# One pool of three PSUM banks for dense products and layer norms, in place of two and one

## The chip, the cores and the metric

The kernel runs on one core of a Trainium2 chip. Its time is the device time of one execution, in microseconds (us); of the kernel before it is the median of three runs. The core's engines are TensorE (PE in the rows; PEld is its weight load), VectorE (DVE), ScalarE (ACT), GpSimd (POOL) and SyncE (SP), which here issues the DMAs. TensorE writes its results to PSUM, which this kernel divides into eight banks of 128 partitions by 512 fp32 values.

## The reference

Two layers, each made of a half-step SwiGLU, a token mixer, and a second half-step SwiGLU. Behind each of the three stands a layer norm, and that is the part of the reference that this change touches.

```python
def layer_norm(x, g, b):
    xf = x.astype(jnp.float32)
    mu = xf.mean(-1, keepdims=True)
    var = jnp.square(xf - mu).mean(-1, keepdims=True)
    return ((xf - mu) * lax.rsqrt(var + LN_EPS)).astype(x.dtype) * g + b

def swiglu(h, w_in, w_out):
    gate, up = jnp.split(h @ w_in, 2, axis=-1)
    return (jax.nn.silu(gate) * up) @ w_out

    # in reference(), h is (1, 576, 1024), of which 528 rows are live
    for l in range(DEPTH):                                    # DEPTH = 2
        h = layer_norm(DEEPNORM_ALPHA * h + 0.5 * swiglu(h, w_ff1_in[l], w_ff1_out[l]), ln_g[l, 0], ln_b[l, 0])
        mix = hybrid_mixer(h * valid, w_in[l], w_out[l], ...)  # 4 DeltaNet, 4 RWKV-7 and 4 retention heads
        h = layer_norm(DEEPNORM_ALPHA * h + mix, ln_g[l, 1], ln_b[l, 1])
        h = layer_norm(DEEPNORM_ALPHA * h + 0.5 * swiglu(h, w_ff2_in[l], w_ff2_out[l]), ln_g[l, 2], ln_b[l, 2])
```

## The kernel before

The 528 live tokens are cut into two halves of 272 and 256. Activations lie with the model dimension on the partitions, so a half is a tile `h` of 128 x 8 x 272 or 256. All work on a half is cut into units. A dense unit (`gate`, `up`, `ffo` of the SwiGLU; `qkv`, `rw`, `rt`, `z`, `ba`, `out` of the mixer) loads a 512 KB slab of weights (`raw`, four buffers), splits it into a high and a low fp32r part (`whl`, three buffers; ScalarE writes the high part at L127, VectorE the low part at L115), and runs 24 matmuls at L165 into one PSUM bank (18 where the slab is smaller): high by high, high by low and low by high, for up to eight slices of 128. This is called a product below. Then ScalarE and VectorE read the bank and so set it free: `gate` by a tanh and a `scalar_tensor_tensor` that writes `m`, `up` by a multiply with `m`, `ffo` and `out` by a `scalar_tensor_tensor` that adds to `h`.

The layer norm of a half is the function `layer_norm`. GpSimd has summed the eight slices of `h` into `acc` (`add_r`). One matmul with a matrix of ones makes the sums for the mean (`pmean`); four instructions of VectorE subtract the mean from `h`; ScalarE squares; VectorE and GpSimd add the squares (`sq`); four small matmuls make the variance (`pvar`); ten short VectorE instructions make the reciprocal root and a last one the diagonal matrix `diag`; one matmul spreads that over the partitions (`prs`); then VectorE and ScalarE scale `h` and write its high and low parts `hi` and `lo`, 16 instructions on VectorE. There are twelve layer norms: three for each layer and half. The last one of the second half has an `end` form, which leaves the last slice of `acc` to a second matmul and no work to GpSimd.

The banks: the dense products take theirs from `psA` (two), the three results of the layer norm from `psL` (one), the mixer's small products from `psB` (two) and `psC` (three).

What sets the order: the program is written as a sequence of units of both halves (`go`, `mix`, `turns`), so that units of one half stand behind a layer norm of the other. A scheduler then lays the instructions out for each engine when the kernel is built. A matmul can be laid out only once the pool of its tile has a bank free. On the chip each engine works through its own list.

Of the kernel before, what the change touches and what calls it, by code (L numbers as in the profile page):

```python
# [14 lines left out]
PSUM = bass.MemoryType.PSUM  # L15
# [44 lines left out]
def body(ctx, tc, xT, w1i, w1o, w2i, w2o, win, wba, wout, par, wsm, wupx, cst, tab, out):  # L60
# [7 lines left out]
    wh = ctx.enter_context(tc.tile_pool(name="whl", bufs=3))  # L68
    wk = ctx.enter_context(tc.tile_pool(name="work", bufs=1))
    st = ctx.enter_context(tc.tile_pool(name="state", bufs=1))  # L70
    psA = ctx.enter_context(tc.tile_pool(name="psA", bufs=2, space=PSUM))
    psL = ctx.enter_context(tc.tile_pool(name="psL", bufs=1, space=PSUM))
    psB = ctx.enter_context(tc.tile_pool(name="psB", bufs=2, space=PSUM))
    psC = ctx.enter_context(tc.tile_pool(name="psC", bufs=3, space=PSUM))
    dr = ctx.enter_context(tc.tile_pool(name="dram", bufs=1, space=DRAM))
# [1276 lines left out]
```

## Time and profile before

| | us |
|---|---|
| median of three runs (2446.88 to 2451.85) | 2447.68 |
| the profiled execution's own time | 2447.37 |
| its span, first to last instruction | 2445.5 |
| TensorE busy in the span | 2387.8 |
| VectorE busy | 1817.1 |
| ScalarE busy | 1226.5 |
| GpSimd busy | 293.7 |

The mean granted clock of TensorE is 0.993 of 2.4 GHz. The rows below come from one profiled execution. A row of the chain of waits gives a start in us, a length in us and what ran. A line such as L165 is that of a helper which many places call, so the names of the tiles tell what an instruction belongs to. A matmul of fp32 (`pmean`, `pvar`, `prs`) shows as two rows, so that 12 layer norms show 24 rows of `pmean`.

### The profile page before, as it was taken

How to read it: one execution, taken by the hardware profiler on the slowest of the kernel's cores; microseconds unless marked ns; L12 is line 12 of the kernel's file. 1: busy time of each engine (PE TensorE's matmuls, PEld its weight loads, DVE VectorE, ACT ScalarE, POOL GpSimd, SP SyncE). 2: the span in 40 equal slices, each digit the busy share in tenths (PEclk: the TensorE clock that was granted, in tenths of full speed). 3: DMA queues.
4: the chain of work that ended last, by engine and by line, in shares of the span. 5: the costliest groups of instructions: out<-in, count | busy, mean ns of one | idle time of the engine just before them, and what ended most of it. 6: DMA issues, size and time to landing. Idle time of an engine off the chain costs nothing.

```text
span 2445.5 us, 51826 instructions
## 1 busy us (share of the span) xinstructions
PE 2387.8 (98%) x20058; PEld 2285.6 (93%) x20058; DVE 1817.1 (74%) x4325; ACT 1226.5 (50%) x2813; POOL 293.7 (12%) x492
## 2 busy tenths in 40 slices
PE   9999999999899999999999999999999999999997
PEld 9999999889899989999999998889998989999997
DVE  6658688768888656976667679976688886687667
ACT  5445555434665334554445556633556653355444
POOL 1001112202222000300001003210022220010002
PEclk9999999999999999999999999999999999999998
DMA  7655554424544525555555544343455445255554
GB/s 248 207 166 172 182 165 134 130 90 157 174 156 150 144 87 172 178 171 179 179 179 172 191 159 153 118 121 107 163 174 190 156 143 154 93 194 170 194 168 127
DMA packets 169821, 389.24 MB, mean 159 GB/s; under 512 B 63750, under 2 KB 79720, under 8 KB 168936
## 3 DMA queue, kind: packets, MB, share of 16 engines
q1 hardware_dynamic: 169576, 385.94, 49.2%
q8 instruction: 158, 2.59, 0.4%
q14 instruction: 87, 0.71, 0.1%
HBM read 372.01 MB, written 13.88 MB: 158 GB/s over the span
## 4 chain that ended last, share of the span: by engine, by line
PE 89%; DVE 6%; DMA 2%; ACT 1%; issue 1%; POOL 1%; SPq 0%; POOLq 0%; DVEq 0%; ACTq 0%
PE up L165 20%; PE ffo L165 20%; PE gate L165 20%; PE qkv L165 6%; PE rw L165 3%; PE out L165 3%; PE rt L165 2%; DVE whl L115 2%; PE po L130 1%; DVE h L118 1%; PE z L165 1%; PE pR L130 1%; PE pyr L130 1%; PE pS L130 1%; PE pz L130 1%
## 5 line engine op out<-in xcount | busy, mean ns | idle before, releaser
L127 ACT ACTIVATE whl<-raw 128x512 fp32r<-128x512 f32 x1384 | 780.1, 614 | 620.6 <-issue 223.3
L115 DVE TENSOR_TENSOR whl<-raw,whl 128x512 fp32r<-128x512 f32 x1384 | 940.5, 710 | 94.4 <-ACT whl L127 79.4
L165 PE MATMUL gate<-hi,whl 128*128 128x256 f32 (+1 forms) x2816 | 553.3, 287 | 6.2 <-DVE m L118 4.0
L165 PE MATMUL up<-hi,whl 128*128 128x256 f32 (+1 forms) x2816 | 553.4, 287 | 2.7 <-DVE m L115 1.2
L165 PE MATMUL ffo<-ghi,whl 128*128 128x256 f32 (+1 forms) x2816 | 529.8, 286 | 5.4 <-DVE h L118 5.2
L165 PEld LDWEIGHTS gate<-hi,whl 128*128 128x128 f32 x2816 | 449.2, 189 | 13.7 <-DVE m L118 5.1
L165 PEld LDWEIGHTS up<-hi,whl 128*128 128x128 f32 x2816 | 450.6, 189 | 8.6 <-issue 3.7
L165 PEld LDWEIGHTS ffo<-ghi,whl 128*128 128x128 f32 x2816 | 440.4, 188 | 11.8 <-DVE h L118 6.4
L165 PE MATMUL up<-lo,whl 128*128 128x256 f32 (+1 forms) x1408 | 403.3, 286 | 0.0
L165 PE MATMUL gate<-lo,whl 128*128 128x256 f32 (+1 forms) x1408 | 402.0, 285 | 0.7 <-DVE lo L115 0.7
L165 PE MATMUL ffo<-glo,whl 128*128 128x256 f32 (+1 forms) x1408 | 399.2, 284 | 0.0
L165 PEld LDWEIGHTS gate<-lo,whl 128*128 128x128 f32 x1408 | 265.4, 188 | 3.8 <-issue 1.6
L165 PEld LDWEIGHTS up<-lo,whl 128*128 128x128 f32 x1408 | 266.4, 189 | 2.6 <-issue 1.2
L165 PEld LDWEIGHTS ffo<-glo,whl 128*128 128x128 f32 x1408 | 264.8, 188 | 0.9 <-issue 0.2
L127 ACT ACTIVATE tanh<-gate 128x256 f32<-128x256 f32 (+1 forms) x176 | 68.2, 387 | 229.8 <-PE gate L165 229.7
L118 DVE SCALAR_TENSOR_TENSOR m<-tanh,gate 128x256 f32<-128x256 f32 (+1 forms) x176 | 74.6, 424 | 139.5 <-ACT tanh L127 138.6
L118 DVE SCALAR_TENSOR_TENSOR h<-ffo,h 128x256 f32<-128x256 f32 (+1 forms) x192 | 81.5, 427 | 99.6 <-PE ffo L165 98.8
L165 PE MATMUL qkv<-hi,whl 128*128 128x272 f32 (+1 forms) x768 | 152.3, 290 | 1.6 <-ACT rk L127 1.6
L115 DVE TENSOR_TENSOR m<-m,up 128x256 f32<-128x256 f32 (+1 forms) x176 | 74.6, 424 | 95.7 <-PE up L165 95.3
L165 PEld LDWEIGHTS qkv<-hi,whl 128*128 128x128 f32 x768 | 122.4, 188 | 4.4 <-ACT rk L127 2.4
L165 PE MATMUL qkv<-lo,whl 128*128 128x272 f32 (+1 forms) x384 | 109.3, 285 | 0.0
L165 PE MATMUL out<-yhi,whl 128*128 128x256 f32 (+1 forms) x512 | 95.8, 285 | 4.6 <-DVE h L118 3.1
(316 smaller groups left out, 3271.1 us busy)
## 6 DMA issues: line engine op xcount, KB each, us to landing
raw<-w1i SPq DMA_DIRECT2D x176, 512.0 KB, 3.4
raw<-w2i SPq DMA_DIRECT2D x176, 512.0 KB, 3.3
raw<-win SPq DMA_DIRECT2D x116, 512.0 KB, 3.3
raw<-w1o SPq DMA_DIRECT2D x64, 512.0 KB, 3.3
raw<-w2o SPq DMA_DIRECT2D x64, 512.0 KB, 3.3
raw<-wout SPq DMA_DIRECT2D x32, 512.0 KB, 4.3
raw<-w1o SPq DMA_DIRECT2D x32, 384.0 KB, 3.0
raw<-w2o SPq DMA_DIRECT2D x32, 384.0 KB, 3.1
```

The costliest lines, as they stand in the source:

```text
L115: e.tensor_tensor(out=o, in0=a, in1=b, op=op)
L118: V.scalar_tensor_tensor(out=o, in0=a, scalar=s, in1=b, op0=op0, op1=op1)
L127: A.activation(out=o, in_=a, func=f, **kw)
L130: PE.matmul(o, lhsT=l, rhs=r, start=start, stop=stop)
L165: PE.matmul(ps, lhsT=w[:, a, k, :m], rhs=x[b][:, k, :n], start=(i == 0), stop=(i == 3 * nk - 1))
```

## The change

The pool `psL` goes away as a pool of its own: the name now stands for `psA`, which has three banks instead of two. The sum stays eight banks. The layer norm's three tiles (`pmean`, `pvar`, `prs`) and a few matmuls at the very start ask for their banks in the same pool as the dense products.

```diff
-    psA = ctx.enter_context(tc.tile_pool(name="psA", bufs=2, space=PSUM))
-    psL = ctx.enter_context(tc.tile_pool(name="psL", bufs=1, space=PSUM))
+    psA = psL = ctx.enter_context(tc.tile_pool(name="psA", bufs=3, space=PSUM))
     psB = ctx.enter_context(tc.tile_pool(name="psB", bufs=2, space=PSUM))
     psC = ctx.enter_context(tc.tile_pool(name="psC", bufs=3, space=PSUM))
```

No instruction is added or removed, but the lists change. Since the diff is one line shorter, line numbers of the changed kernel are one less (L129 for L130, L164 for L165).

TensorE's list at the first layer norm (first layer, half of 272), before: the matmul of the mean stands inside an `up` product of the other half.

```order
L165 MATMUL up<-hi,whl 128x256 x2
L165 MATMUL up<-lo,whl 128x256
L130 MATMUL pmean<-acc,ones 128x272
L165 MATMUL up<-hi,whl 128x256 x2
L165 MATMUL up<-lo,whl 128x256
```

It stands 32 matmuls behind the last `ffo` product that it follows from: a `gate` of 24 and eight of this `up` have been laid between.

Further down the same list, before, the matmul that spreads the root: it is the first thing between an `up` and a `gate` product. Between `pmean` and it the list has 160 matmuls of dense products.

```order
L165 MATMUL up<-hi,whl 128x256 x2
L165 MATMUL up<-lo,whl 128x256
L165 MATMUL up<-hi,whl 128x256
L130 MATMUL prs<-diag,ones 128x272
L165 MATMUL gate<-hi,whl 128x256
L165 MATMUL gate<-lo,whl 128x256
```

The variance's four matmuls stand in between in the same way, inside another `up`.

The same layer norm in TensorE's list of the changed kernel, from the last matmuls of the `ffo` products that it normalises.

```order
L164 MATMUL ffo<-ghi,whl 128x272 x2
L164 MATMUL ffo<-glo,whl 128x272
L164 MATMUL ffo<-ghi,whl 128x272
L129 MATMUL pmean<-acc,ones 128x272
L129 MATMUL pvar<-ones,sq 68x1 x4
L129 MATMUL prs<-diag,ones 128x272
L164 MATMUL gate<-hi,whl 128x256
L164 MATMUL gate<-lo,whl 128x256
```

The three kinds of matmul now stand one behind the other, with no dense product between them; the 160 matmuls stand behind `prs`. It is so at ten of the twelve layer norms. At the seventh (first layer, second SwiGLU, half of 256) thirteen small matmuls of the mixer stand between them and no dense product. The twelfth, the last work of the kernel, had nothing between them before either.

VectorE's list at the same layer norm, before, from the subtraction of the mean to the first adding of squares: splits of weights (`whl`) and work on products of the other half (`m`, `glo`) stand between.

```order
L118 SCALAR_TENSOR_TENSOR h<-pmean,h 128x544 x4
L115 TENSOR_TENSOR whl<-raw,whl 128x512
L115 TENSOR_TENSOR m<-m,up 128x256
L115 TENSOR_TENSOR whl<-raw,whl 128x512 x2
L115 TENSOR_TENSOR sq<-sq 128x544
L115 TENSOR_TENSOR glo<-m,ghi 128x256
L118 SCALAR_TENSOR_TENSOR m<-tanh,gate 128x256
```

The layer norm's steps and those of the other half alternate.

The same place in the changed kernel, from the last `ffo` result on.

```order
L117 SCALAR_TENSOR_TENSOR h<-ffo,h 128x272
L114 TENSOR_TENSOR whl<-raw,whl 128x512 x2
L117 SCALAR_TENSOR_TENSOR h<-pmean,h 128x544 x4
L114 TENSOR_TENSOR sq<-sq 128x544 x2
L114 TENSOR_TENSOR sq<-sq 128x272
L123 TENSOR_SCALAR var<-pvar 68x4
```

From the mean to `diag` VectorE's list holds nothing but this layer norm. Then come its 16 scaling instructions, and only behind them the first work on a dense product:

```order
L114 TENSOR_TENSOR diag<-cst,ry 68x272
L117 SCALAR_TENSOR_TENSOR h<-h,par_228,prs 128x272 x8
L117 SCALAR_TENSOR_TENSOR lo<-h,par_228,hi 128x272 x8
L117 SCALAR_TENSOR_TENSOR m<-tanh,gate 128x256
L114 TENSOR_TENSOR whl<-raw,whl 128x512 x2
```

The work on dense products, which was mixed in before, has moved behind all of these.

## Rows read from the trace of the kernel before

**Rows 1.** The page, its first lines: span, and busy time of each engine.

```profile
span 2445.5 us, 51826 instructions
PE 2387.8 (98%) x20058; PEld 2285.6 (93%) x20058; DVE 1817.1 (74%) x4325; ACT 1226.5 (50%) x2813; POOL 293.7 (12%) x492
```

**Rows 2.** The page, the chain that ended last: shares of the span by engine.

```profile
PE 89%; DVE 6%; DMA 2%; ACT 1%; issue 1%; POOL 1%; SPq 0%; POOLq 0%; DVEq 0%; ACTq 0%
```

**Rows 3.** Waits of TensorE: who for whom; us in total, times, longest us.

```profile
PE ffo L165 <- DVE h L118: 5.2, 9, 2.6
PE rt L165 <- DVE rt L115: 4.9, 3, 3.0
PE gate L165 <- DVE m L118: 4.0, 5, 1.7
PE out L165 <- DVE h L118: 3.1, 6, 1.0
PE up L165 <- DVE m L115: 1.2, 2, 0.6
```

**Rows 4.** Timeline of TensorE, 457.5 to 464 us: start, length, what, wait before.

```profile
457.93 0.40 PE L165 MATMUL gate<-hi,whl 128*128 128x256 f32 x2
461.07 0.71 PE L130 MATMUL pb<-kap,rk 128*128 128x128 f32 x4 [2.74 <-POOL kap L115]
...
463.60 0.58 PE L165 MATMUL gate<-lo,whl 128*128 128x256 f32 x1
```

**Rows 5.** Chain of waits through the first layer norm, 205 to 250 us.

```profile
212.15 0.46 PE pmean L130 x2
...
224.88 0.43 PE pvar L130 x8
...
232.28 0.47 PE prs L130 x2
```

**Rows 6.** Timeline of the last layer norm, 2424 us to the end.

```profile
2427.05 0.59 PE L130 MATMUL pmean<-acc,ones 128*128 128x256 f32 x2
2427.25 0.42 DVE L118 SCALAR_TENSOR_TENSOR h<-ffo,h 128x256 f32<-128x256 f32 x1 [1.71 <-PE ffo L165]
2427.73 0.70 PE L130 MATMUL pmean<-h,ones 128*128 128x256 f32 x2
2428.54 2.48 DVE L118 SCALAR_TENSOR_TENSOR h<-pmean,h 128x512 f32<-128x512 f32 x4 [0.86 <-PE pmean L130]
...
2430.94 2.65 DVE L115 TENSOR_TENSOR sq<-sq 128x512 f32<-128x512 f32 x4
...
2433.74 0.98 PE L130 MATMUL pvar<-ones,sq 128*64 128x1 f32 x8 [5.31 <-DVE sq L115]
...
2437.24 1.19 PE L130 MATMUL prs<-diag,ones 64*128 64x256 f32 x2 [2.51 <-DVE diag L115]
```

**Rows 7.** By tile: times ns min/median/max, first and last start us, forms.

```profile
L115 POOL TENSOR_TENSOR acc<-acc,h x71: 728/784/2213, 197.8 to 2425.7; 128x256 f32<-128x256 f32 x47, 128x272 f32<-128x272 f32 x24
L118 DVE SCALAR_TENSOR_TENSOR h<-pmean,h x48: 677/682/718, 212.8 to 2430.3; 128x512 f32<-128x512 f32 x32, 128x544 f32<-128x544 f32 x16
L118 DVE SCALAR_TENSOR_TENSOR h<-h,par,prs x80: 465/475/498, 232.8 to 2202.4; 128x256 f32<-128x256 f32 x48, 128x272 f32<-128x272 f32 x32
```

**Rows 8.** VectorE's groups, 205 to 250 us: busy us, mean ns of one.

```profile
L115 DVE TENSOR_TENSOR whl<-raw,whl 128x512 fp32r<-128x512 f32 x30 | 22.1, 769 | 0.9 <-ACT whl L127 0.5
L118 DVE SCALAR_TENSOR_TENSOR lo<-h,par,hi 128x272 fp32r<-128x272 f32 x8 | 3.6, 497 | 0.0
L118 DVE SCALAR_TENSOR_TENSOR m<-tanh,gate 128x256 f32<-128x256 f32 x6 | 2.5, 416 | 0.7 <-ACT tanh L127 0.7
```

**Rows 9.** Dense products in three stretches: length, TensorE busy, granted clock, DMA.

```profile
461.90:468.70 6.80, 5.10 (x24) 0.50 0.74 179
1854.50:1857.90 3.40, 3.40 (x18) 0.50 0.62 193
2300.00:2310.00 10.00, 10.00 (x87) 1.00 0.55 184
```

## The prediction

> **What bounds the kernel now.** I read the busy times first. TensorE is busy for 2387.8 of a span of 2445.5 us, VectorE for three quarters of it, the others less [rows 1]. The chain of waits says the same: 89% of it lies on TensorE, 6% on VectorE [rows 2]. So what doesn't stop TensorE costs nothing, and what stops it costs its full length; all idle time of TensorE together is 2445.5 - 2387.8 = 57.7 us, a ceiling on what any change of banks can win.
>
> Next, which waits of TensorE end when a bank of the dense products comes free. Those are the waits of a product for the VectorE instruction that reads an earlier product: 5.2, 4.9, 4.0, 3.1 and 1.2 us, 18.4 us in 25 waits [rows 3]. That is what a third bank can go after.
>
> Last, whether TensorE passes over a matmul that must wait. It doesn't: in the middle of a gate product a small matmul, pb, waited 2.74 us for GpSimd, and the rest of the same gate product, which had all it needed, ran only behind it [rows 4]. What stands first in TensorE's list stops all that stands behind it.
>
> **What the change adds.** In the lists of the changed kernel the three steps of a layer norm (mean, variance, spreading) stand one behind the other on TensorE, with no dense product between them. I take the reason to be the shared pool: a later product gets no bank before the layer norm's third tile, which is written earlier, has got its own. For the time only the list counts. Each step needs the result of VectorE's or GpSimd's work on the step before, so TensorE now stands still through the whole layer norm. Before, dense products of the other half filled this: at the first layer norm 20.1 us passed from the mean (212.15) to the spreading (232.28) with TensorE at work throughout [rows 5].
>
> What one such stop lasts is shown by the last layer norm, the one that had no products beside it before [rows 6]:
> - From the end of the dense products (2427.05, where the first mean matmul starts) to the second mean matmul 0.68 us pass (2427.73): VectorE adds the last product to h. The other layer norms also have GpSimd's add to acc there, 0.78 us [rows 7]. Together 1.46 us.
> - From the mean to the variance 6.01 us (2427.73 to 2433.74): four subtractions, squares and sums.
> - From the variance to the spreading 3.50 us (2433.74 to 2437.24): eleven short instructions and the diagonal.
> - The spreading itself holds TensorE for 0.47 us at full clock [rows 5]; the clock is low by then, so about twice that, 0.94 us.
>
> That is 11.91 us. Of it the three steps cost TensorE 0.46 + 0.43 + 0.47 = 1.36 us before too [rows 5], so 10.55 us are new. Eleven layer norms pay it (the twelfth stands as before): 116.1 us. Four of the eleven are on the half of 272; the subtraction takes 718 ns there against 677 [rows 7], and at this ratio each loses about 0.35 us more: 1.4 us. At the sixth VectorE's list still holds two splits of weights and one other dense step inside, 2 x 0.77 + 0.42 us [rows 8]: 2 us. At the seventh it holds some twenty instructions of the mixer, most of them short: I take 4 us. The sum is 123.5 us.
>
> The bounds of one stop: not under the 10.55 us of a layer norm that had VectorE to itself, less the 0.78 if GpSimd's add hides behind a late product, so 9.8; not over the 20.1 us of the first layer norm, where VectorE had dense work in between, with the ends added and the old cost taken off 20.1 + 1.46 + 0.94 - 1.36 = 21.1. I take the lower end, because VectorE's list holds nothing else there, except at the two named.
>
> **The clock.** A stop also costs clock. After the longest wait of an rt product, 3.0 us [rows 3], which ended at 1853.8 us, TensorE was granted 0.50, the lower of its two levels (1.2 GHz), for 3.4 us; after the 2.74 us of [rows 4] it was 6.8 us. In 3.4 us at the lower level 18 products' matmuls ran, where 8.7 for each us, 29.6, run at the full one [rows 9]: 11.6 are lost, and at 0.115 us each that is 1.3 us; for 6.8 us 2.7 us. Stops of 11 us are longer than all of these, so I expect one such loss behind each. With 2.0 us, the middle, eleven make 22 us; the ends are 15 and 30.
>
> **What follows a stop.** Behind the spreading VectorE's list has 16 scaling instructions before it serves a product: 8 x 0.475 and 8 x 0.497 us [rows 7, 8], 7.8 us; then 0.42 us for the first gate and 1.54 us for the split of the next weights. That is 9.7 us. TensorE has three slabs of weights split and ready: the first product takes about 24 / 5.3 = 4.5 us at the lower clock (18 in 3.4 us is 5.3 for each us), two more 2 x 24 / 8.7 = 5.5 us, so it asks for the fourth at 10.0 us. The cover is 0.3 us; I cost this at nothing, and come back to it as a rival.
>
> **What the change gives back.** Between layer norms the products have three banks. I count all 18.4 us of bank waits as gone, and with them the half clock behind the longest of them, 1.3 us: -20 us, rounded. Many of these waits stand around layer norms, where VectorE had to serve both at once; there they go because TensorE stands still instead. The bounds are 0 and the whole 57.7 us.
>
> The Trainium skill, page "TensorE: Matmul & The Clock Gate", section "HAM oscillation — how this bites in real kernels", reports a kernel in which double-buffering PSUM gave no further gain once the order kept TensorE busy; by this the 20 us would be 0, and the time 2593. The trace here names 18.4 us of waits on just such banks, so I keep the term, but the upper part of my range allows for it.
>
> **The sum.** 123.5 + 22 - 20 = +125.5 us on the profiled execution's 2447.37 us (its span is 2445.5, the rest lies around it): 2572.9, so 2573 us. The median of the three runs, 2447.68, is 0.3 us from that execution, and shifts nothing.
>
> **The rivals.**
> - The cover behind the stop is too thin. If VectorE is some 3 us late with the fourth slab and the bank behind it, each stop grows by that: +33 us, 2606. For it: the 0.3 us above. Against it: behind this point VectorE needs four splits and three other steps for a gate and an up, 4 x 0.77 + 3 x 0.42 = 4.3 us, where TensorE needs 48 / 8.7 = 5.5 us, so it catches up. Chance 0.16.
> - More comes back: TensorE's stop lets VectorE and ScalarE, who fall behind in the mixers, catch up, and most of the 57.7 us of idle time goes. That is up to 37.7 us more than counted: 2535. Against it: 5.31 + 2.51 = 7.8 us of that idle time is the last layer norm [rows 6], which stays, and the 2.74 us of [rows 4] are on GpSimd. Chance 0.13.
> - The stop is as long as the first layer norm's 20.1 us. Then each lasts 20.1 - 6.01 - 3.50 = 10.6 us more: 2690. For it would speak a late split of weights ahead of the subtraction (two stand there in the list). Chance 0.03.
> - The other side: TensorE isn't held, and the third bank does what banks do. Then only the -20 us remain: 2427, faster. It is decided at the eleven places where the variance matmul waits: it holds if products behind it run in the meantime. The 2.74 us of [rows 4] speak against it. The Trainium skill, page "Perfetto Trace Analysis", section "Optimization Strategy", would have this outcome, since it reads a repeated gap on the engine that should be saturated as a sign of too few buffers; the gaps of [rows 3] are such, but they are small beside the stops. Chance 0.02.
> - My forecast has the rest, 0.66, with its own range of 2546 to 2600.
>
> **Numbers.** A difference of 0.2%, 5 us, is about what a measurement of this kernel can tell from none. The range from 2535 to 2608 leaves out the third and the fourth rival and about half of the first and of the second: 0.03 + 0.02 + 0.08 + 0.06 = 0.19. Faster has 0.02, no change 0.01 (an unlikely mix of the last rival with a part of the stops), slower 0.97.
>
> **What would show it.** In the profile after: TensorE's waits led by the variance matmul on VectorE's sum (eleven times and more, each 5 us or so), the spreading on the diagonal (2 to 3 us each) and the mean on GpSimd's add (1 us or so); TensorE busy nearly as long as before in a span some 125 us longer, so about 93%; a mean granted clock under 0.98, with half-clock stretches behind the layer norms; and the waits of [rows 3] mostly gone. I am wrong in the mechanism if dense matmuls run between the mean and the spreading, and wrong in a size if a stop is far from 12 us, if the lower clock lasts much longer than 6.8 us behind it, or if the fourth product waits for its weights.

## The result, and the profile after

The changed kernel takes 2557.36 us (median of 4 runs, 2555.80 to 2557.69), the kernel before 2448.64 us in runs beside it (4 runs, 2446.88 to 2451.85). The ratio is 1.0436, 95% interval 1.0423 to 1.0449: slower by 108.7 us. The forecast was 2573, with a range of 2535 to 2608.

The page of the changed kernel, its span and busy times, and the chain that ended last by engine:

```profile
span 2555.1 us, 51918 instructions
PE 2415.5 (95%) x20058; PEld 2310.2 (90%) x20058; DVE 1821.2 (71%) x4325; ACT 1229.0 (48%) x2813; POOL 282.1 (11%) x492
...
PE 91%; DVE 5%; ACT 2%; issue 1%; DMA 1%; POOL 1%; SPq 0%; POOLq 0%; DVEq 0%; ACTq 0%
```

Against [rows 1] the span grew by 109.6 us. TensorE's idle time went from 57.7 to 2555.1 - 2415.5 = 139.6 us, and its busy time grew by 27.7 us although it runs the same 20058 matmuls. The mean granted clock fell from 0.993 to 0.965. The chain [rows 2] hardly differs, and its shares do not show this cost.

TensorE's waits in the changed kernel (who for whom; us in total, times, longest us):

```profile
PE pvar L129 <- DVE sq L114: 64.5, 12, 7.0
PE prs L129 <- DVE diag L114: 26.8, 11, 2.5
PE pmean L129 <- POOL acc L114: 19.4, 10, 3.4
...
PE pyt L954 <- DVE yn L114: 3.2, 1, 3.2
PE ffo L164 <- DVE h L117: 2.6, 2, 2.0
PE pot L746 <- DVE on L114: 2.2, 1, 2.2
...
PE out L164 <- ACT yhi L126: 1.7, 1, 1.7
```

The three steps of the layer norm lead with 110.7 us. Of the bank waits in [rows 3], 18.4 us, only 2.6 us are left. All that TensorE waits for outside the layer norm is 139.6 - 110.7 = 28.9 us; it was 57.7 less the last layer norm's 7.8 [rows 6] and less the 1.2 that one mean had waited for GpSimd, 48.7 us. The rows `pot`, `pyt` and `out` for `yhi` are new: 7.1 us at one place, the end of the second layer's last mixer, of which more below.

TensorE's timeline through the first layer norm (start, length, what, wait before). In [rows 5] the same three steps stood 20.1 us apart with TensorE at work; here it stops:

```profile
209.31 0.72 PE L129 MATMUL pmean<-acc,ones 128*128 128x272 f32 x2 [2.06 <-POOL acc L114]
215.49 1.07 PE L129 MATMUL pvar<-ones,sq 128*68 128x1 f32 x8 [5.46 <-DVE sq L114]
219.03 1.28 PE L129 MATMUL prs<-diag,ones 68*128 68x272 f32 x2 [2.47 <-DVE diag L114]
```

The spaces, 6.18 and 3.54 us, are those of the last layer norm before, 6.01 and 3.50 [rows 6]. The last `ffo` matmul started at 206.96 and the next `gate` at 219.72: the stop is 12.76 us.

The stop and the stretch behind it in windows (length, then busy us and instructions of PE, PEld, DVE, ACT, POOL, then granted clock, DMA share, GB/s), as [rows 9]:

```profile
206.96:219.72 12.76, 2.77 (x15) 1.92 (x14) 9.35 (x22) 3.70 (x6) 2.64 (x4) 0.63 0.36 119
219.72:224.00 4.28, 4.28 (x21) 4.16 (x20) 3.65 (x9) 3.06 (x8) 0.00 (x0) 0.50 0.00 0
...
224.00:234.00 10.00, 10.00 (x86) 10.00 (x86) 8.64 (x19) 8.42 (x20) 0.00 (x0) 1.00 0.43 149
```

Behind the stop TensorE ran 4.28 us at the lower of its two levels, 21 matmuls, and then at the full rate of 86 in 10 us. The instructions inside the stop are slower too: 0.72, 1.07 and 1.28 us, where the timeline of the kernel before has 0.62, 0.60 and 0.62 for the same three.

### The profile page after: what moved, and what is told of

It reads as the page before. It is cut to its first block, busy times and chain, and to the rows that moved or that the text cites. A ratio compares the mean times of both kernels' runs of the same rounds, so it can differ in the third digit from the quotient of the medians.

```text
span 2555.1 us, 51918 instructions
## 1 busy us (share of the span) xinstructions
PE 2415.5 (95%) x20058; PEld 2310.2 (90%) x20058; DVE 1821.2 (71%) x4325; ACT 1229.0 (48%) x2813; POOL 282.1 (11%) x492
## 4 chain that ended last, share of the span: by engine, by line
PE 91%; DVE 5%; ACT 2%; issue 1%; DMA 1%; POOL 1%; SPq 0%; POOLq 0%; DVEq 0%; ACTq 0%
PE gate L164 20%; PE up L164 20%; PE ffo L164 18%; PE qkv L164 6%; PE out L164 4%; PE rw L164 3%; PE rt L164 3%; PE z L164 2%; DVE whl L114 2%; PE po L129 1%; ACT sq L126 1%; PE pR L129 1%; DVE sq L114 1%; DVE h L117 1%; PE pyr L129 1%
## 5 line engine op out<-in xcount | busy, mean ns | idle before, releaser
L164 PE MATMUL gate<-hi,whl 128*128 128x256 f32 (+1 forms) x2816 | 560.6, 290 | 0.0
L164 PE MATMUL up<-hi,whl 128*128 128x256 f32 (+1 forms) x2816 | 550.7, 287 | 0.1
L164 PE MATMUL ffo<-ghi,whl 128*128 128x256 f32 (+1 forms) x2816 | 529.1, 286 | 3.3 <-DVE h L117 2.6
L164 PEld LDWEIGHTS gate<-hi,whl 128*128 128x128 f32 x2816 | 456.2, 192 | 7.6 <-issue 4.9
L164 PEld LDWEIGHTS up<-hi,whl 128*128 128x128 f32 x2816 | 449.3, 189 | 5.7 <-issue 2.8
L164 PEld LDWEIGHTS ffo<-ghi,whl 128*128 128x128 f32 x2816 | 440.8, 189 | 9.0 <-issue 3.4
L164 PE MATMUL gate<-lo,whl 128*128 128x256 f32 (+1 forms) x1408 | 406.0, 288 | 0.5 <-DVE lo L114 0.5
L164 PE MATMUL up<-lo,whl 128*128 128x256 f32 (+1 forms) x1408 | 402.7, 286 | 0.0
L164 PE MATMUL ffo<-glo,whl 128*128 128x256 f32 (+1 forms) x1408 | 400.4, 286 | 0.0
L164 PEld LDWEIGHTS gate<-lo,whl 128*128 128x128 f32 x1408 | 269.4, 191 | 2.6 <-DVE lo L114 0.9
L164 PEld LDWEIGHTS up<-lo,whl 128*128 128x128 f32 x1408 | 265.7, 189 | 2.8 <-issue 2.0
L164 PEld LDWEIGHTS ffo<-glo,whl 128*128 128x128 f32 x1408 | 265.9, 189 | 1.1 <-issue 0.4
L117 DVE SCALAR_TENSOR_TENSOR m<-tanh,gate 128x256 f32<-128x256 f32 (+1 forms) x176 | 74.7, 425 | 150.9 <-ACT tanh L126 150.4
L117 DVE SCALAR_TENSOR_TENSOR h<-ffo,h 128x256 f32<-128x256 f32 (+1 forms) x192 | 81.1, 426 | 109.4 <-PE ffo L164 108.8
L164 PE MATMUL qkv<-hi,whl 128*128 128x272 f32 (+1 forms) x768 | 148.3, 286 | 0.0
L164 PEld LDWEIGHTS qkv<-hi,whl 128*128 128x128 f32 x768 | 122.0, 189 | 1.5 <-issue 1.2
L164 PE MATMUL qkv<-lo,whl 128*128 128x272 f32 (+1 forms) x384 | 110.2, 287 | 0.0
L164 PE MATMUL out<-yhi,whl 128*128 128x256 f32 (+1 forms) x512 | 98.6, 293 | 4.4 <-ACT whl L126 2.1
```

What stands on the lines that cost most here:

```text
L117: V.scalar_tensor_tensor(out=o, in0=a, scalar=s, in1=b, op0=op0, op1=op1)
L164: PE.matmul(ps, lhsT=w[:, a, k, :m], rhs=x[b][:, k, :n], start=(i == 0), stop=(i == 3 * nk - 1))
```

## The experiments

Theory A, that of the prediction: requests to a pool are laid out in the order in which they are written, so a later product gets no place in TensorE's list before the layer norm's last request has its own; TensorE then waits at the head of its list. Rivals were what the shared pool does in other ways: that fewer banks are free, or that the layer norm's tiles hold them too long. Below, a stretch's "loss" is its length less what its matmuls take at their median spacing in the kernel before; I matched the traces matmul by matmul for it, and call the sum of these losses the ledger. A layer norm's stretch starts with the last dense matmul ahead of its mean and holds its stop and the matmuls that follow, some 45 us in all at that spacing; where it is taken to end moves its loss by up to 2 us.

**One request for each layer norm** (edit of the changed kernel).

```diff
-        pm = bank(psL, "pmean")
+        pln = bank(psL, "pln")
+        pm = pln
...
-        pv = bank(psL, "pvar")
+        pv = pln[:, 384:388]
...
-        pb = bank(psL, "prs")
+        pb = pln
```

> The changed kernel, but mean, variance and spreading use one tile, so that a layer norm makes one request of the shared pool of three. Dense products stand behind the mean in TensorE's list. Theory A: only the wait for the mean is left, about 2 us at eleven layer norms (22 us), and what came back stays only as far as the third bank gave it. If the third bank gave back all of the 20 us that the prediction counted: 2448 + 22 - 20 = 2450; if the stops themselves gave it back by letting VectorE rest: about 2470. Rival B (three banks are too few for both, so products wait while a layer norm holds one for some 15 us): slower than before by the waits of two banks and by the mean, 2470 to 2490.

Measured: 2456.75 us (10 runs), ratio 1.0023 (1.0011 to 1.0035). In TensorE's list the dense products come back right behind the mean; of the waits inside the eleven layer norms hardly more than the one there is left, 23.4 us, and it is the first of the waits (the row for `sq` is the last layer norm's):

```profile
PE pln L129 <- POOL acc L114: 23.4, 10, 4.4
PE pln L129 <- DVE sq L114: 5.2, 1, 5.2
```

So 100.6 of the 108.7 us hang on the variance and the spreading standing ahead of the dense products in TensorE's list. It is A's outcome, between its two values. The trace is of the slowest of the ten executions, 2462.78 us.

**Two requests, variance and spreading in one tile** (`pm` keeps its own).

```diff
-        pv = bank(psL, "pvar")
+        pln = bank(psL, "pvarprs")
+        pv = pln[:, 384:388]
...
-        pb = bank(psL, "prs")
+        pb = pln
```

> The changed kernel, but variance and spreading share one tile, so that a layer norm asks the shared pool for two tiles and the last request is made for the variance. In TensorE's list dense products then stand from the variance on; mean and variance still stand one behind the other. Theory A (a later product gets no bank before the layer norm's last request is served, and TensorE stands still until then): at ten layer norms the stop loses its last part, which lasted from the variance to the next product 3.43 + 1.15 us or so in the changed kernel, about 4.2 us with the variance's own time taken off: 2557 - 42 = 2515 us, 2500 to 2525. Rival B (the layer norm's tiles fill the three banks, whatever the order of requests): as the changed kernel or slower, 2550 to 2565, since the shared tile is held longer.

Measured: 2532.26 us, ratio 1.0324 (1.0309 to 1.0340). The waits:

```profile
PE pvarprs L129 <- DVE sq L114: 64.4, 12, 7.0
PE pmean L129 <- POOL acc L114: 19.5, 10, 3.5
...
PE pvarprs L129 <- DVE diag L114: 2.4, 1, 2.4
```

The waits for `diag` went from 26.8 to 2.4 us and nothing else in these rows moved. The direction is A's; the size, 25 us, is under the 42 that I expected of it, and the time lies above A's range of 2500 to 2525. At the first six layer norms the loss fell from 87.8 to 69.2 us, some 3 each. The stops themselves shortened as A has it: from the last dense matmul to the next product the eleven now last 104.8 us in all, 40.8 less, of which about 5 are the spreadings, which now run outside them. About 10 us were lost again outside the stops. There VectorE's work on products is mixed in with the layer norm again from the variance on, but no run shows that this took them.

**Two requests, mean and variance in one tile** (`prs` keeps its own). This has the same number of requests as the run above, in another place.

```diff
-        pm = bank(psL, "pmean")
+        pln = bank(psL, "pmeanvar")
+        pm = pln
...
-        pv = bank(psL, "pvar")
+        pv = pln[:, 384:388]
```

> The kernel after, with pmean and pvar in one tile and prs in its own: two requests of the pool for each layer norm instead of three, as in the run that joined pvar and prs (2532). Theory A (requests are served in the order written; dense products come back in TensorE's list behind the layer norm's last request, which here is still that of prs): the three steps still stand together, the stop is as long as in the kernel after, and the time is 2557, within 2550 to 2563. Rival B (what costs is the number of requests, or how long the layer norm's tiles hold banks): two requests cost the same wherever they stand, so 2532 as with the other pair, within 2525 to 2540.

Measured: 2557.23 us, ratio 1.0432 (1.0417 to 1.0448), the time of the changed kernel, and its waits to the decimal:

```profile
PE pmeanvar L129 <- DVE sq L114: 64.5, 12, 7.0
PE prs L129 <- DVE diag L114: 26.8, 11, 2.5
PE pmeanvar L129 <- POOL acc L114: 19.4, 10, 3.4
```

Equal counts of requests, 25 us apart: what decides is where the last request stands, not how many there are. Rival B falls.

**The shared pool with two banks**, one bank of PSUM left unused.

```diff
-    psA = psL = ctx.enter_context(tc.tile_pool(name="psA", bufs=3, space=PSUM))
+    psA = psL = ctx.enter_context(tc.tile_pool(name="psA", bufs=2, space=PSUM))
```

> The changed kernel with two banks in the shared pool instead of three; one bank of PSUM stays unused. TensorE's list has the same three steps without products between. Theory A: the eleven stops stay as they are. If the third bank gives back what came back in the changed kernel (some 40 to 50 us against the kernel before), this one is slower by 20 to 40 us: 2577 to 2597. If the stops themselves give it back, by letting VectorE and ScalarE catch up: 2555 to 2565. The stall at the end of the last mixer, 15 us at 2230 us in the changed kernel, should be absent if it comes from dense products that a third bank let run ahead.

Measured: 2557.93 us, ratio 1.0431 (1.0415 to 1.0447): the same as with three. Its waits:

```profile
PE pvar L129 <- DVE sq L114: 62.4, 12, 7.0
PE prs L129 <- DVE diag L114: 25.8, 11, 2.6
PE pmean L129 <- POOL acc L114: 18.9, 10, 2.6
...
PE ffo L164 <- DVE h L117: 1.6, 6, 0.3
...
PE up L164 <- DVE m L114: 1.2, 2, 0.6
PE gate L164 <- DVE m L117: 1.1, 1, 1.1
...
PE rt L164 <- DVE rt L114: 0.8, 1, 0.8
...
PE out L164 <- DVE h L117: 0.6, 2, 0.3
```

With two banks the bank waits are 1.6 + 1.2 + 1.1 + 0.8 + 0.6 = 5.3 us: 13.1 of the 18.4 us of [rows 3] go without a third bank. That they were there because VectorE served a layer norm and products at once is my reading; no run shows it by itself. The waits at the mixer's end are absent, as expected.

The equal time does not mean that the third bank does nothing beside the stops. The mean of the sixth layer norm and that of the tenth, in the changed kernel:

```profile
1378.71 0.62 PE L129 MATMUL pmean<-acc,ones 128*128 128x272 f32 x2
...
2265.57 0.70 PE L129 MATMUL pmean<-acc,ones 128*128 128x256 f32 x2 [1.38 <-POOL acc L114]
```

and with two banks:

```profile
1387.72 0.62 PE L129 MATMUL pmean<-acc,ones 128*128 128x272 f32 x2
...
2261.66 0.70 PE L129 MATMUL pmean<-acc,ones 128*128 128x256 f32 x2 [1.39 <-POOL acc L114]
```

At the sixth, three banks are 9.0 us ahead (1.7 at the first); at the tenth, behind the second layer's last mixer, 3.9 us behind.

**The third bank for the products alone** (edit of the kernel before: the layer norm's tiles go to the mixer's pool).

```diff
-    psA = ctx.enter_context(tc.tile_pool(name="psA", bufs=2, space=PSUM))
-    psL = ctx.enter_context(tc.tile_pool(name="psL", bufs=1, space=PSUM))
+    psA = ctx.enter_context(tc.tile_pool(name="psA", bufs=3, space=PSUM))
...
-    psC = ctx.enter_context(tc.tile_pool(name="psC", bufs=3, space=PSUM))
+    psC = psL = ctx.enter_context(tc.tile_pool(name="psC", bufs=3, space=PSUM))
```

> The kernel before with a third bank for the dense products; the layer norm takes its banks from the mixer's pool of three instead of one of its own. So the third bank stands without the shared pool of dense products and layer norms, and dense products stand between mean and spreading as before. Theory A: no stop, so not slower than before; if the third bank gives back the bank waits (18.4 us and half clock behind them) 2415 to 2432, if what came back was due to the stops 2440 to 2450. Rival B (third bank itself makes the list worse): slower than before by more than 20 us.

Measured: 2432.68 us, ratio 0.9914 (0.9895 to 0.9933): faster than before by 19 us. So a third bank for the products, with the layer norm in the mixer's pool, is worth about what the prediction's last term said, 20 us, and the waits of [rows 3] are gone from its list. The waits at the end of the second layer's last mixer stand in its list as well:

```profile
PE pyt L954 <- DVE yn L114: 3.9, 1, 3.9
...
PE pot L746 <- DVE on L114: 2.2, 1, 2.2
PE out L164 <- ACT yhi L126: 1.7, 1, 1.7
```

**TensorE kept at work inside the stops** (edit of the changed kernel; the added matmuls write a bank that nobody reads).

```diff
+        pd = bank(psC, "idle")
...
+            for i in range(0 if end else 5):
+                mm(pd[:, :128], ones, hv[:, k, :128])
...
+        for i in range(0 if end else 10):
+            mm(pd[:, :128], ones, sq[:, 0, :128])
```

> The kernel after, with matmuls whose results nobody uses inside the eleven stops: five of 128 columns in fp32 behind each subtraction of the mean and ten behind the last sum of squares, into a bank of the mixer's pool. They do no work for the layer norm; they keep TensorE busy while it waits. Theory A (each stop also costs the lower clock behind it, 41 us at half clock in all, of which 18 to 19 us are lost): the mean granted clock rises from 0.965 to 0.98 or more, the half-clock stretches behind the stops go, and the time is 2539, within 2533 to 2546. Rival B (TensorE's lower clock behind a stop costs nothing, since the products there wait for weights or banks anyway): the clock rises, the time stays at 2555 to 2562. A third way: the added matmuls stand in the way of the variance and the spreading and each stop grows by a part of a us; then up to 2565.

Measured: 2551.98 us (2546.78 to 2553.41), ratio 1.0413 (1.0396 to 1.0430); mean granted clock 0.986. The first layer norm in TensorE's timeline, and the stretch behind it in a window (columns as above):

```profile
210.04 0.72 PE L129 MATMUL pmean<-acc,ones 128*128 128x272 f32 x2 [2.06 <-POOL acc L114]
211.58 6.34 PE L129 MATMUL idle<-h,ones 128*128 128x128 f32 x40 [0.82 <-DVE h L117]
217.76 0.60 PE L129 MATMUL pvar<-ones,sq 128*68 128x1 f32 x8
...
220.83 0.73 PE L129 MATMUL prs<-diag,ones 68*128 68x272 f32 x2
```

```profile
221.19:225.49 4.30, 4.30 (x37) 4.26 (x36) 3.89 (x10) 3.26 (x8) 0.00 (x0) 1.00 0.00 0
```

Behind the stop 37 matmuls ran in 4.30 us, where the changed kernel ran 21 in 4.28: 16 at 0.115 us, 1.8 us. Over all eleven stops the loss in the first 12 us' worth of matmuls behind a stop fell from 22.2 to 5.0 us. That is the term of the clock, 17 us of it. The time fell by less: the added matmuls stood in the way of the variance, which now comes 7.72 us behind the mean instead of 6.18, and the stops together grew by 5.1 us. The median lies outside A's range of 2533 to 2546. Both the first and the third way of the expectation are in it; B, that the clock costs nothing, is not. The profiled execution (2546.78 us, the shortest of the four) is 10.4 us under the changed kernel's, the median 5.4; why the other three are longer I have no trace of.

**Cover for the mixer's end** (edit of the changed kernel). In the second layer TensorE's list ends the last mixer, before, with `pot` and then `pyt` and `pgate`, between 48, 63 and 33 matmuls of `ffo`; after, with 36 of `ffo`, then `pot`, `pyt`, `pgate` and the `out` products in a row. The edit moves three units ahead:

```diff
-            ah, c2 = 46, 56
+            ah, c2 = 49, 56
```

The place in the changed kernel's timeline, without the edit:

```profile
2230.79 0.89 PE L746 MATMUL pot<-cst,on 128*128 128x128 f32 x4 [2.21 <-DVE on L114]
2234.90 0.69 PE L954 MATMUL pyt<-cst,yn 128*128 128x128 f32 x2 [3.22 <-DVE yn L114]
2238.46 1.01 PE L164 MATMUL out<-yhi,whl 128*128 128x256 f32 x3 [1.72 <-ACT yhi L126]
```

> The kernel after, with one number of the order changed (ah from 46 to 49): in the second layer three more units of the second SwiGLU's first half stand ahead of the second half's output products, so that in TensorE's list a gate product now covers the last steps of the mixer (pot, pyt, pgate), where the kernel after has nothing. Theory A (the third bank let the covering ffo products run early, and the bare end of the mixer costs 11 us over the kernel before, the lower clock behind it included): 2547, within 2542 to 2551. Rival B (those steps wait for VectorE's or ScalarE's backlog, not for cover; the wait moves to the output products): 2555 to 2560.

Measured: 2552.09 us (2550.78 to 2553.63), ratio 1.0412 (1.0396 to 1.0427). The waits between 2200 and 2260 us:

```profile
PE out L164 <- ACT yhi L126: 2.0, 1, 2.0
PE out L164 <- DVE ylo L114: 0.4, 1, 0.4
```

`pot` and `pyt` no longer wait, and the median is 5.3 us lower; the intervals of the two ratios overlap by their ends (1.0423 and 1.0427), so the waits that went say more than the time. The wait for `yhi` stayed, as B had it. The median lies between the two ranges. So A is half right: by the medians some 5 of its 11 us are the lost cover.

**The same edit on the third bank for the products alone.**

```diff
-            ah, c2 = 46, 56
+            ah, c2 = 49, 56
```

> The kernel before with three banks for the dense products and the layer norm in the mixer's pool of three (2432.7 when run), and with ah at 49 instead of 46 as in the run beside it. Theory A: the same bare mixer end of some 10 us goes here too: 2423, within 2419 to 2427, ratio to the kernel before 0.987 to 0.990. Rival B: no change, 2430 to 2435.

Measured: 2428.70 us (2426.00 to 2432.06), ratio 0.9909 (0.9894 to 0.9923). It beats the kernel before; against the version without the edit (0.9895 to 0.9933) nothing is shown. Its profiled span is 2424.2 us with `pot` and `pyt` gone from the waits, but 1.8 us of `gate` for `hi` have come in, and those for `lo` at L117 grew from 0.8 to 1.5.

## Why the prediction was right, and where it was not

**The mechanism of the stop** was right at every step: no dense matmul runs between the mean and the spreading, the waits are the three named, in the order named, and the runs with one and two requests show that the place of the last request in the list sets the stop.

**The stops: right.** Predicted 123.5 us new. From the last dense matmul to the next product the eleven stops last 145.6 us in all (12.0 to 14.2 each, the seventh 18.2 with the mixer's thirteen matmuls inside); taking off what their matmuls took before leaves 125.4. The last layer norm of the kernel before, which had VectorE to itself, was the right measure, and the 20.1 us of [rows 5] the wrong one. Single extras were off: the sixth, for which I added 2 us, waits 7.0 us for the squares as I thought, but its mean does not wait at all, and its stop is the shortest, 12.0 us. The seventh lost 12.5 us with the clock behind it, about the mean of the others; the 4 us added there were not needed. The other nine lost 11.3 us each where the sum had 10.7 without the extras, above all since the mean came later: 2.1 us from the end of the dense products in the mean, in place of 1.46. So the sum is as close as it is by luck: extras that were not needed stood in for a part that was too small. The third rival did not come: from the mean to the spreading no stop takes more than 13.8 us, where that rival had 20.1.

**The clock: right, within its bounds of 15 and 30.** Predicted 22 us, measured 22.2 behind the stops. Of these 17.2 went when TensorE was kept at work, and only so much is shown to be the clock's; the other 5.0 stayed, in part waits of `rot` for `rq` (2.4 us in the changed kernel).

**The cover behind a stop: right.** No `gate` or `up` waits for `whl` or for a bank in the changed kernel, though 0.3 us is all the cover I found; in the 20 us behind a stop no product waits for weights. The first rival did not come.

**What is given back: the term that was mis-sized.** Predicted 20 us, from the waits of [rows 3]. Stops and the loss behind them cost 147.6 us, the span grew by 109.6, so 38.0 us came back net of the new waits at the mixer's end. Two things were wrong in that term.
- Its cause. I gave it to the third bank. With two banks the time is the same, so most of it comes without that bank, beside the stops: in the lists VectorE finishes a layer norm alone, and then serves products alone. The third bank for the products alone does bring 19 us. With the layer norms held it adds nothing in sum: it was 9.0 us ahead at the sixth layer norm, and lost this and more by the tenth, for the most part at the mixer's end.
- Its size. Bank waits were only a part of what the overlap cost. Outside the eleven stops and the last layer norm TensorE's idle time fell from 42.7 to 19.8 us. So of the 38.0 us net, 22.9 came out of idle time and the other 15.1 out of time that counts as busy. By the ledger the stretches of the first six layer norms lost 26.7 us before; after, 5.0 us beyond the stops and the loss right behind them; with two banks 6.0; with the third bank for the products alone 14.5 in all. What it looks like in the kernel before, behind the first spreading, against the changed kernel behind its stop:

```profile
232.00:242.00 10.00, 8.25 (x68) 7.97 (x67) 9.64 (x22) 9.61 (x22) 0.00 (x0) 1.00 0.33 107
242.00:252.00 10.00, 9.04 (x76) 8.86 (x75) 7.31 (x16) 5.64 (x13) 0.00 (x0) 1.00 0.90 318
```

```profile
234.00:244.00 10.00, 10.00 (x87) 10.00 (x86) 6.98 (x13) 5.20 (x12) 0.00 (x0) 1.00 0.81 278
244.00:254.00 10.00, 10.00 (x86) 10.00 (x86) 6.26 (x13) 5.09 (x11) 0.00 (x0) 1.00 0.53 168
```

Before, 144 matmuls in 20 us with VectorE and ScalarE at over 9.6 of the first 10; after, 173. These windows do not hold the same matmuls. Matched one by one, the 144 behind the first spreading took 21.3 us before and 17.9 in the changed kernel, 3.4 us less, of which [rows 3] counts 1.7 (the longest wait of `gate` for `m`) as a bank wait; another 1.0 us was a wait for split weights, and the rest lay in time that counts as busy. With two shared banks the 144 take 17.9 us too, and with the third bank for the products alone about 18: at this place either way gives the same back. The second rival (more comes back, since VectorE and ScalarE catch up) came nearest, with about half of its extra 37.7 us: 18.0. That the catching up is the cause was argued from the lists and these windows, not tested.

**The mixer's end: not foreseen.** With three banks the list lets `ffo` products run early that had covered the last steps of a mixer. With two shared banks the list has the 48, 63 and 33 `ffo` matmuls in their old places and none of these waits, so it is the third bank that does it. It costs some 11 us over the kernel before by the ledger; moving three units ahead of its end returned 5.3. Without this the give-back would be 43 to 49 us. So the forecast is as near as 16 us partly by luck: the give-back was put too low, and a cost that I had not seen took some of the difference away. With two shared banks other waits stand in the list (`pG` 4.1 us); I did not follow these.

The other side, the fourth rival at 2427, is what the third bank gives when the products have it to themselves (2432.7). As a forecast of this change it was wrong for the reason given: the requests are served in written order. The Trainium skill, page "Perfetto Trace Analysis", section "Optimization Strategy", says that repeated gaps on the engine that should be saturated can mean too few buffers. The runs bear that out only for a pool of the products' own: a third bank shared with the layer norm made the gaps of [rows 3] go and the kernel 4.36% slower. The other case that the prediction weighed is in the Trainium skill's page "TensorE: Matmul & The Clock Gate", section "HAM oscillation — how this bites in real kernels": one kernel in which double-buffering PSUM gave no further gain. This kernel differs where the products have the banks to themselves: 19 us came of the third. With the layer norms held, two and three banks tie at 2557.9 and 2557.4, but as the sum of a gain and a loss.

What stays open: which part of VectorE's and ScalarE's work the give-back consists of (no run moved it by itself), what took back some 10 us outside the shortened stops of the run with variance and spreading in one tile, and the second half of the bare mixer's end.

## What to carry to other kernels

Before merging pools, look in the engines' lists at what is written between the first and the last request of a chain whose steps wait for another engine: in the shared pool of this kernel independent work was laid no earlier than behind the chain's last request. If a bank must be shared, let such a chain take one tile for all its steps, or share with work that isn't the cover (here the mixer's pool: 0.9914 against 1.0436 for the same third bank). And when an overlap is taken away, don't size what comes back by idle time alone: here some 15 of 38 us came back out of time that had counted as busy.
